# Batched 64x64 matmul on one core: transposing A on VectorE in 32x32 blocks instead of on TensorE

## The chip, the cores and the metric

The kernel runs on one core of one Trainium2 chip. The metric is the device time of one execution in microseconds (us). Three runs of the kernel before gave 134.71, 134.80 and 134.83 us, a median of 134.8 us.

## The reference

1024 independent products of 64x64 matrices in fp32:

```python
a: [1024, 64, 64] float32      # M x K
b: [1024, 64, 64] float32      # K x N
out = np.matmul(a, b)          # [1024, 64, 64] float32
```

16.78 MB of A and 16.78 MB of B are read, and 16.78 MB are written.

## The kernel before

**Tiling.** The work goes in 16 tiles (t) of 64 matrices, each 1 MB of A, of B and of output. A is prepared in 8 superblocks (s) of 128 matrices, so one superblock feeds two tiles. The matrices of a tile are numbered 4g + h, with g from 0 to 15 and h from 0 to 3. Inside the kernel A and B are bf16, and two neighbouring bf16 of A (k = 2kp and 2kp + 1) are moved together as one fp32 word.

**How a product is made.** TensorE multiplies four matrices (h = 0..3) at once: the stationary operand is a block diagonal `at_bd` whose 128 rows are (h, kp) and whose 128 columns are (wl, h', mo), with zeros where h and h' differ. The moving operand is `b_bf`, rows (h, kp), 64 columns. `multiply(t)` (from L158, matmuls at L189) does 64 matmuls a tile: 16 values of g, two of j, and two (u = 0, 1) that add the even and the odd k. Row m of A is m = 4 mo + 2j + wl. Two block diagonals (`N_BD = 2`) take turns; their zeros are written once, one by VectorE (L217), the other in halves by GpSimd (L219, L222).

**How A gets into the block diagonal.** Four steps per superblock:

- `load_a(s)` (L69 to L78): three of the four h are loaded by GpSimd's queue with a cast to bf16 (L73, 128 partitions, 4 KB runs of DRAM, 2 KB in SBUF); the fourth is loaded as fp32 on SP's queue (L77). Superblock 0 comes as fp32 in four parts on SP's and ScalarE's queues (`load_first_a`, L80 to L91).
- `regroup(s)` (L99 to L113): VectorE puts the four h side by side in `a_bf`, one copy of 3072 bf16 (L108) and one cast of 1024 fp32 (L111) per superblock. For s = 0 VectorE and ScalarE share it (L105).
- `transpose(s, j)` (L115 to L126): TensorE transposes 128x128 fp32 words against an identity, four to a PSUM tile (L120), and ScalarE copies each PSUM tile to `at_sb` (L123). That is 16 transposes and 4 copies a superblock.
- `spread(t)` (L128 to L138): VectorE copies 32 partitions at a time from `at_sb` into the block diagonal, 1024 words each (L133), four copies a tile.

**B and the output.** `load_b(t)` (L93 to L97) loads 1 MB of fp32, even tiles on SP's queue, odd ones on ScalarE's, three buffers. `cast(t)` (L140 to L152) makes `b_bf`, two buffers: VectorE does it (L144), except tile 0 (ScalarE) and tile 15 (four pieces, two on each engine, L149 and L151). The products are copied from PSUM to `o_sb` in eight pieces of 64x512 a tile (`evacuate`, L177): ScalarE does all eight on even tiles, six on odd ones, where VectorE does the other two. Tile 15 is done in pieces of 256, half on each engine. `store` (L166) puts 1 MB a tile on GpSimd's queue; tiles 14 and 15 go in pieces on SP's and ScalarE's queues.

**What sets the order.** The order is written out by hand (`manual_schedule`): each engine runs its instructions in the order in which the program names them, and waits at each for what it needs. On VectorE an iteration t is `spread(t+1)`, `cast(t+1)`, then its share of the evacuation and, in every second iteration, `regroup(s+2)`. GpSimd's queue holds the loads of A and the stores in one order; at most eight of its DMAs are outstanding, since each waits for the landing of the one eight before it. A is loaded up to three superblocks ahead (`A_AHEAD = 3`), B three tiles, and a tile is stored one iteration after its evacuation (`HOLD = 2`).

Of the kernel before, what the change touches and what calls it, by code (L numbers as in the profile page):

```python
# [7 lines left out]

fp32 = mybir.dt.float32
# [4 lines left out]
def kernel(  # L14
# [7 lines left out]

    nc = tc.nc
    B, M, K = a.shape  # L30
    _, _, N = b.shape
    assert (M, K, N) == (64, 64, 64) and B % 128 == 0

    n_t, n_s = B // 64, B // 128
    A_AHEAD = 3
    B_AHEAD = 3
    N_BD = 2
    HOLD = 2

    a_v = a.rearrange("(s g h) (mp v) k -> s h g mp (v k)", h=4, g=32, v=16)  # L40
    b_v = b.rearrange("(t g h) (kp u) n -> t (h kp) g (u n)", h=4, g=16, u=2)
# [3 lines left out]
    a_pool = ctx.enter_context(tc.tile_pool(name="a_pool", bufs=A_AHEAD))  # L45
    b_pool = ctx.enter_context(tc.tile_pool(name="b_pool", bufs=B_AHEAD))
    work = ctx.enter_context(tc.tile_pool(name="work", bufs=2))
    o_pool = ctx.enter_context(tc.tile_pool(name="o_pool", bufs=8))
    t_psum = ctx.enter_context(
        tc.tile_pool(name="t_psum", bufs=4, space=bass.MemoryType.PSUM)  # L50
    )
    o_psum = ctx.enter_context(
        tc.tile_pool(name="o_psum", bufs=2, space=bass.MemoryType.PSUM)
    )

    bd_tiles = [
        consts.tile([128, 2, 16, 2, 4, 16], fp32, name=f"at_bd{i}") for i in range(N_BD)
    ]
    identity = consts.tile([128, 128], fp32)
    warm = consts.tile([128, 2], fp32)  # L60
    a_tiles, b_tiles, abf_tiles, at_tiles, bbf_tiles = {}, {}, {}, {}, {}
    held = {}

    def store_queue(t, lo):
        if t < n_t - 2:
            return nc.gpsimd
        return nc.scalar if t == n_t - 1 and lo % 4 == 0 else nc.sync

    def load_a(s):  # L69

        a_sb = a_pool.tile([128, 3, 16, 64], bf16, name="a_sb")
        for h in range(3):
            nc.gpsimd.dma_start(  # L73
                out=a_sb[:, h, :, :].rearrange("p v k -> p (v k)"), in_=a_v[s, h], single_packet=True
            )
        a_raw = a_pool.tile([128, 16, 64], fp32, name="a_raw")
        nc.sync.dma_start(out=a_raw[:].rearrange("p v k -> p (v k)"), in_=a_v[s, 3])  # L77
        a_tiles[s] = a_sb, a_raw  # L78

    def load_first_a():  # L80

        raw = [
            o_pool.tile([128, 8, 2, 2, 64], fp32, name="o_sb")[:].rearrange(
                "p gh j wl n -> p (gh j wl n)"
            )
            for _ in range(2)
        ]
        parts = [raw[h % 2][:, 1024 * (h // 2) : 1024 * (h // 2) + 1024] for h in range(4)]
# [10 lines left out]
    def regroup(s):  # L99
        a_sb = a_tiles.pop(s)  # L100
        a_bf = work.tile([128, 16, 4, 64], bf16, name="a_bf")
        if s == 0:
            for h in range(4):
                copy = nc.scalar.copy if h % 2 else nc.vector.tensor_copy
                copy(a_bf[:, :, h, :], a_sb[h].rearrange("p (v k) -> p v k", v=16))  # L105
        else:
            cast_sb, raw = a_sb
            nc.vector.tensor_copy(  # L108
                a_bf[:, :, 0:3, :], cast_sb[:].rearrange("p h v k -> p v h k")
            )  # L110
            nc.vector.tensor_copy(a_bf[:, :, 3, :], raw[:])  # L111
        abf_tiles[s] = a_bf
        at_tiles[s] = work.tile([128, 2, 32, 2, 4, 4], fp32, name="at_sb")  # L113

    def transpose(s, j):  # L115
        a_cols = abf_tiles[s][:].rearrange("p v h k -> p v (h k)").bitcast(fp32)
        for wl in range(2):
            at_ps = t_psum.tile([128, 4, 128], fp32, name="at_ps")
            for vo in range(4):
                nc.tensor.transpose(  # L120
                    at_ps[:, vo, :], a_cols[:, 4 * vo + 2 * j + wl, :], identity[:]
                )
            nc.scalar.copy(  # L123
                at_tiles[s][:, j, :, wl, :, :],
                at_ps[:].rearrange("p vo (g mp) -> p g mp vo", mp=4),
            )  # L126

    def spread(t):  # L128
        half = slice(16 * (t % 2), 16 * (t % 2) + 16)
        bd = bd_tiles[t % N_BD]  # L130
        for h in range(4):
            rows = slice(32 * h, 32 * h + 32)
            nc.vector.tensor_copy(  # L133
                bd[rows, :, :, :, h, :].rearrange("p j g wl mo -> p j (g wl) mo"),
                at_tiles[t // 2][rows, :, half, :, :, :].rearrange(
                    "p j g wl mp vo -> p j (g wl) (mp vo)"
                ),
            )  # L138

    def cast(t):  # L140
# [15 lines left out]
            piece()  # L156

    def multiply(t):  # L158
        at_bd = bd_tiles[t % N_BD][:].rearrange("p j g wl h mo -> p j g (wl h mo)")
        at_bd = at_bd.bitcast(bf16).rearrange("p j g (c u) -> p j g c u", u=2)  # L160
        b_bf = bbf_tiles.pop(t)
        last = t == n_t - 1
# [6 lines left out]
            )  # L169

        def evacuate(o_ps, gh, n, copies):

            for par in range(2):
                for wl in range(2):
                    src = o_ps[64 * wl : 64 * wl + 64, :, par, :, :]
                    dst = o_sb[64 * par : 64 * par + 64, gh : gh + n, :, wl, :]
                    copies[2 * par + wl](dst, src)  # L177

        for half in range(2):
            if not last:  # L180
                o_ps = o_psum.tile([128, 4, 2, 2, 64], fp32, name="o_ps")
            for g8 in range(8):
                if last and g8 % 4 == 0:
                    o_ps = t_psum.tile([128, 2, 2, 2, 64], fp32, name="at_ps")
                g = 8 * half + g8
                gl = (g8 % 4 if last else g8) // 2
                for j in range(2):
                    for u in range(2):
                        nc.tensor.matmul(  # L189
                            o_ps[:, gl, g % 2, j, :],  # L190
                            at_bd[:, j, g, :, u],
                            b_bf[:, g, 64 * u : 64 * u + 64],
                            start=(u == 0),
                            stop=(u == 1),
                        )
                if last and g8 % 4 == 3:
                    copy = nc.scalar.copy if g8 == 3 else nc.vector.tensor_copy
                    evacuate(o_ps, g // 4 * 2, 2, [copy] * 4)
            if not last:
                copies = [nc.scalar.copy] * 4  # L200
                if half and t % 2:
                    copies[2:] = [nc.vector.tensor_copy] * 2
                evacuate(o_ps, 4 * half, 4, copies)
        if last:
            held[t] = [lambda q=q: put(2 * q, 2) for q in range(4)]
        else:
# [1 line left out]
            held[t] = [lambda q=q: put(q, 8 if whole else 4) for q in ([0] if whole else [0, 4])]  # L208

    with tc.manual_schedule():  # L210
        load_first_a()
# [16 lines left out]
        cast(0)
        for t in range(n_t):
            s, half = t // 2, t % 2  # L230
            if t + 1 < n_t:
                spread(t + 1)
                cast(t + 1)
            if t + B_AHEAD < n_t:
                load_b(t + B_AHEAD)
            if half == 0 and 0 < s < n_s - 1 - A_AHEAD:
                load_a(s + 1 + A_AHEAD)
            if half == 0 and 0 < s < n_s - 1:
                transpose(s + 1, 1)
            multiply(t)  # L240
            if t == 0:
                regroup(1)
                load_a(A_AHEAD)
                load_a(A_AHEAD + 1)
                transpose(1, 0)
                transpose(1, 1)
            elif t == 1:
                regroup(2)
            elif half == 0 and s + 2 < n_s:
                regroup(s + 2)  # L250
            if half == 1 and s + 2 < n_s:
                transpose(s + 2, 0)
# [34 lines left out]
```

## Time and profile before

| what | value |
|---|---|
| median of three runs | 134.8 us |
| span of the profiled execution, first to last instruction | 133.4 us |
| VectorE (DVE) busy | 94.6 us, 71% |
| ScalarE (ACT) busy | 87.9 us, 66% |
| TensorE (PE) busy, of it transposes | 64.4 us, 48%; 21.2 us |
| GpSimd (POOL) busy, mostly issuing DMAs | 33.0 us, 25% |
| DRAM traffic | 33.55 MB read, 16.78 MB written: 377 GB/s over the span |

The page does not give the time of the profiled execution as a run; the 1.4 us between its span and the median of the runs lie before the first and after the last instruction, or are differences between executions.

How to read it: the page gives busy time per engine, the span in 40 slices of 3.3 us with the busy share in tenths, the DMA queues with their packets and bytes, a chain of waits followed back from the last instruction, and the costliest groups of instructions with their mean duration and the idle time before them. DMA bytes are counted as they land, so a load that casts fp32 to bf16 counts half of what it reads. q0 is GpSimd's queue, q1 SP's, q10 ScalarE's. Sizes such as 32x1024 are partitions x elements of one instruction.

### The profile page before, as it was taken

What the parts mean: (1) busy time and instruction counts of PE and PEld (TensorE: products, weight loads), DVE (VectorE), ACT (ScalarE), POOL (GpSimd) and SP (SyncE); (2) the same over time, 40 slices, a digit from 0 to 9 for tenths busy, and PEclk for the clock granted to TensorE, in tenths of its full rate; (3) what the DMA queues carried; (4) which work ended last, traced back from release to release, by engine and by line L of the source; (5) the groups of instructions that cost most, each with busy time, mean ns of one, the idle gap of its engine ahead of it and who ended that gap; (6) DMA issues with size and microseconds to landing.
All of it is one profiled execution on the core that took longest, in us unless ns stands there. A gap on an engine that the chain in (4) does not pass through costs nothing.

```text
span 133.4 us, 2837 instructions
## 1 busy us (share of the span) xinstructions
PE 64.4 (48%) x1152; PEld 61.1 (46%) x1152; DVE 94.6 (71%) x120; ACT 87.9 (66%) x161; POOL 33.0 (25%) x43
## 2 busy tenths in 40 slices
PE   0006406960089384289518970956197363970000
PEld 0006306950089274189418950945196363960000
DVE  5930399109998809995999699959999995987000
ACT  3225424999036998969595969696968969099600
POOL 8991000420090070341233021203020410300000
PEclk9999975797557999856985699599959955599555
DMA  3999999999999999999999999999999999999990
GB/s 77 371 329 311 307 311 281 284 306 325 327 312 401 316 320 333 399 384 397 311 281 375 406 389 351 304 316 390 394 396 387 396 392 391 402 405 398 382 319 18
DMA packets 19021, 45.01 MB, mean 337 GB/s; under 512 B 1088, under 2 KB 3136, under 8 KB 19008
## 3 DMA queue, kind: packets, MB, share of 16 engines
q0 software_dynamic: 6832, 20.19, 50.1%
q1 hardware_dynamic: 7120, 14.68, 30.4%
q10 hardware_dynamic: 5056, 9.96, 19.7%
q8 instruction: 9, 0.15, 0.4%
q14 instruction: 4, 0.03, 0.1%
HBM read 33.55 MB, written 16.78 MB: 377 GB/s over the span
## 4 chain that ended last, share of the span: by engine, by line
DMA 53%; DVE 15%; ACT 13%; PE 6%; issue 5%; SPq 2%; DVEq 0%; ACTq 0%
DMA b_sb<-in_b_dram 53%; ACT o_sb L177 9%; DVE at_bd L133 6%; PE o_ps L189 4%; DVE b_bf L144 4%; DVE o_sb L177 3%; PE at_ps L120 2%; ACT at_sb L123 2%; ACT b_bf L144 1%; SPq L90 1%; DVE a_bf L108 1%; SPq L96 1%; ACT b_bf L151 1%; DVE a_bf L111 0%; SPq L77 0%
## 5 line engine op out<-in xcount | busy, mean ns | idle before, releaser
L177 ACT COPY o_sb<-o_ps 64x512 f32<-64x512 f32 x106 | 61.5, 580 | 10.3 <-PE o_ps L189 9.0
L189 PEld LDWEIGHTS <-at_bd 128*128 128x128 bf16 x1024 | 42.3, 113 | 39.5 <-DVE b_bf L144 25.7
L189 PE MATMUL o_ps<-b_bf,at_bd 128*128 128x64 bf16 x960 | 42.6, 216 | 35.4 <-DVE b_bf L144 23.4
L133 DVE COPY at_bd<-at_sb 32x1024 f32<-32x1024 f32 x64 | 46.9, 733 | 14.1 <-ACT at_sb L123 11.8
L120 PE MATMUL at_ps<-identity,a_bf 128*128 128x128 f32 x128 | 21.2, 335 | 19.4 <-ACT a_bf L105 11.2
L166 POOL DMA_DIRECT2D out_dram<-o_sb x14 | 15.4, 1097 | 56.9 <-ACT at_sb L123 23.4
L120 PEld LDWEIGHTS at_ps<-identity,a_bf 128*128 128x128 f32 x128 | 19.3, 180 | 19.5 <-issue 19.5
L123 ACT COPY at_sb<-at_ps 128x512 f32<-128x512 f32 x32 | 17.5, 590 | 11.0 <-PE at_ps L120 7.8
L144 DVE CAST b_bf<-b_sb 128x2048 bf16<-128x2048 f32 x14 | 17.8, 1271 | 9.6 <-DMA b_sb<-in_b_dram 9.4
L73 POOL DMA_DIRECT2D a_sb<-in_a_dram x21 | 13.6, 662 | 26.4 <-DVE a_bf L108 19.4
L177 DVE COPY o_sb<-o_ps 64x512 f32<-64x512 f32 x14 | 9.7, 690 | 0.3
L108 DVE COPY a_bf<-a_sb 128x3072 bf16<-128x3072 bf16 x7 | 6.7, 950 | 0.0
L105 ACT CAST a_bf<-o_sb 128x1024 bf16<-128x1024 f32 x2 | 2.1, 1044 | 5.2 <-DMA o_sb<-in_a_dram 5.2
L111 DVE CAST a_bf<-a_raw 128x1024 bf16<-128x1024 f32 x7 | 4.8, 683 | 0.0
L144 ACT CAST b_bf<-b_sb 128x2048 bf16<-128x2048 f32 x1 | 1.9, 1900 | 3.9 <-DMA b_sb<-in_b_dram 3.9
L105 DVE CAST a_bf<-o_sb 128x1024 bf16<-128x1024 f32 x2 | 2.8, 1382 | 1.9 <-DMA o_sb<-in_a_dram 1.9
L217 DVE MEMSET at_bd<- 128x4096 f32 x1 | 3.5, 3472 | 0.8 <-issue 0.8
L177 DVE COPY o_sb<-at_ps 64x256 f32<-64x256 f32 x8 | 3.4, 422 | 0.5 <-PE at_ps L189 0.4
L151 ACT CAST b_bf<-b_sb 128x512 bf16<-128x512 f32 x2 | 1.1, 615 | 3.6 <-DMA b_sb<-in_b_dram 3.6
L177 ACT COPY o_sb<-at_ps 64x256 f32<-64x256 f32 x8 | 2.9, 366 | 0.1
L214 ACT ACT_TABLE_LOAD x1 | 1.3, 1283 | 2.3 <-issue 2.3
L189 PE MATMUL at_ps<-b_bf,at_bd 128*128 128x64 bf16 x64 | 2.0, 193 | 1.0 <-DVE at_bd L133 1.0
(12 smaller groups left out, 6.1 us busy)
## 6 DMA issues: line engine op xcount, KB each, us to landing
out_dram<-o_sb POOLq DMA_DIRECT2D x14, 1024.0 KB, 21.6
a_sb<-in_a_dram POOLq DMA_DIRECT2D x21, 256.0 KB, 16.4
a_raw<-in_a_dram SPq DMA_DIRECT2D x7, 512.0 KB, 18.7
o_sb<-in_a_dram SPq DMA_DIRECT2D x2, 512.0 KB, 5.9
o_sb<-in_a_dram ACTq DMA_DIRECT2D x2, 512.0 KB, 7.1
out_dram<-o_sb SPq DMA_DIRECT2D x2, 512.0 KB, 7.5
out_dram<-o_sb SPq DMA_DIRECT2D x2, 256.0 KB, 7.8
out_dram<-o_sb ACTq DMA_DIRECT2D x2, 256.0 KB, 5.5
```

The source lines that it names most:

```text
L73: nc.gpsimd.dma_start(out=a_sb[:, h, :, :].rearrange("p v k -> p (v k)"), in_=a_v[s, h], single_packet=True)
L105: copy(a_bf[:, :, h, :], a_sb[h].rearrange("p (v k) -> p v k", v=16))
L108: nc.vector.tensor_copy(a_bf[:, :, 0:3, :], cast_sb[:].rearrange("p h v k -> p v h k"))
L111: nc.vector.tensor_copy(a_bf[:, :, 3, :], raw[:])
L120: nc.tensor.transpose(at_ps[:, vo, :], a_cols[:, 4 * vo + 2 * j + wl, :], identity[:])
L123: nc.scalar.copy(at_tiles[s][:, j, :, wl, :, :], at_ps[:].rearrange("p vo (g mp) -> p g mp vo", mp=4),)
L133: nc.vector.tensor_copy(bd[rows, :, :, :, h, :].rearrange("p j g wl mo -> p j (g wl) mo"), at_tiles[t // 2][rows, :, half, :, :, :].rearrange(
L144: (nc.vector.tensor_copy if t else nc.scalar.copy)(b_bf[:], b_sb[:])
L166: store_queue(t, lo).dma_start(out=o_v[t, :, lo : lo + n, :], in_=o_sb[:, lo : lo + n].rearrange("p gh j wl n -> p (gh j wl n)"),)
L177: copies[2 * par + wl](dst, src)
L189: nc.tensor.matmul(o_ps[:, gl, g % 2, j, :], at_bd[:, j, g, :, u], b_bf[:, g, 64 * u : 64 * u + 64], start=(u == 0), stop=(u == 1),)
L217: nc.vector.memset(bd_tiles[0][:], 0.0)
```

## The change

The preparation of A is rewritten, for tiles of 64 matrices:

- **Load.** A tile of A lies as 32 partitions (g, mp) for each q (the former h), at partitions 32q to 32q + 31. One partition holds 32 rows of one matrix: an 8 KB run of DRAM, 4 KB in SBUF after the cast. It is loaded with four DMAs of 32 partitions each. Tile 0 comes as fp32 on SP's and ScalarE's queues and is cast by VectorE and ScalarE, one half each; tiles 1 to 15 all come cast, on GpSimd's queue: 60 DMAs, without `single_packet`. Six tiles are kept ahead (`A_AHEAD = 6`, in tiles now).
- **Transpose.** `regroup`, TensorE's 128 transposes, the identity, ScalarE's 32 copies to `at_sb` and the copies of `spread` go. `spread` is now four VectorE transposes a tile, each on 32 partitions and 1024 fp32 words: 32 blocks of 32x32, from `a_sb` directly into the block diagonal. They read runs of 32 words, and write single words: neighbouring words of a block land 32 bytes (mp) or 1 KB (g) apart.
- **Block diagonal.** Its columns are (w, q, mp, vo), and the stationary operand of a matmul is still a run of 128 words.
- **Evacuation.** ScalarE does all eight copies of every tile but the last; VectorE's share on odd tiles goes. `o_ps` has three buffers instead of two; tile 15 uses a pool of its own (`q_psum`).
- **Order.** GpSimd's queue starts with the loads of tiles 1, 2 and 3, and zeroes the second block diagonal between the loads of tiles 3, 4 and 5, each of which waits for a landing of an earlier one. SP's queue no longer carries loads of A after tile 0. In an iteration the order is `spread(t+1)`, `cast(t+1)`, `load_b(t+3)`, `load_a(t+6)`, `multiply(t)`, `store(t-1)`.

```diff
-    n_t, n_s = B // 64, B // 128
-    A_AHEAD = 3
+    n_t = B // 64
+    A_AHEAD = 6
     B_AHEAD = 3
     N_BD = 2
     HOLD = 2
-    a_v = a.rearrange("(s g h) (mp v) k -> s h g mp (v k)", h=4, g=32, v=16)
+    RAW = (0,)
+    a_v = [
+        [
+            a[64 * t + q : 64 * t + 64 : 4].rearrange("g (mp v) k -> g mp (v k)", mp=2)
+            for q in range(4)
+        ]
+        for t in range(n_t)
+    ]
...
-        consts.tile([128, 2, 16, 2, 4, 16], fp32, name=f"at_bd{i}") for i in range(N_BD)
+        consts.tile([128, 16, 4, 4, 2, 8], fp32, name=f"at_bd{i}") for i in range(N_BD)
...
-    def load_a(s):
-
-        a_sb = a_pool.tile([128, 3, 16, 64], bf16, name="a_sb")
-        for h in range(3):
-            nc.gpsimd.dma_start(
-                out=a_sb[:, h, :, :].rearrange("p v k -> p (v k)"), in_=a_v[s, h], single_packet=True
-            )
-        a_raw = a_pool.tile([128, 16, 64], fp32, name="a_raw")
-        nc.sync.dma_start(out=a_raw[:].rearrange("p v k -> p (v k)"), in_=a_v[s, 3])
-        a_tiles[s] = a_sb, a_raw
+    def load_a(t):
+        if t in RAW:
+            raw = raw_pool.tile([128, 32, 64], fp32, name="a_raw")
+            raw_tiles[t] = raw
+        else:
+            a_tiles[t] = a_pool.tile([128, 32, 64], bf16, name="a_sb")
+        for q in range(4):
+            rows = slice(32 * q, 32 * q + 32)
+            if t in RAW:
+                queue = nc.scalar if t == 0 and q % 2 else nc.sync
+                queue.dma_start(
+                    out=raw[rows].rearrange("p v k -> p (v k)"), in_=a_v[t][q]
+                )
+            else:
+                nc.gpsimd.dma_start(
+                    out=a_tiles[t][rows].rearrange("p v k -> p (v k)"),
+                    in_=a_v[t][q],
+                )
...
     def spread(t):
-        half = slice(16 * (t % 2), 16 * (t % 2) + 16)
         bd = bd_tiles[t % N_BD]
-        for h in range(4):
-            rows = slice(32 * h, 32 * h + 32)
-            nc.vector.tensor_copy(
-                bd[rows, :, :, :, h, :].rearrange("p j g wl mo -> p j (g wl) mo"),
-                at_tiles[t // 2][rows, :, half, :, :, :].rearrange(
-                    "p j g wl mp vo -> p j (g wl) (mp vo)"
-                ),
+        pairs = a_tiles.pop(t)[:].rearrange("p v k -> p (v k)").bitcast(fp32)
+        pairs = pairs.rearrange("p (vo w kp) -> p w vo kp", vo=8, w=4)
+        for q in range(4):
+            rows = slice(32 * q, 32 * q + 32)
+            nc.vector.transpose(
+                bd[rows, :, :, q, :, :].rearrange("p g w mp vo -> p w vo g mp"),
+                pairs[rows],
             )
...
-                copies = [nc.scalar.copy] * 4
-                if half and t % 2:
-                    copies[2:] = [nc.vector.tensor_copy] * 2
-                evacuate(o_ps, 4 * half, 4, copies)
+                evacuate(o_ps, 4 * half, 4, [nc.scalar.copy] * 4)
...
+        load_a(3)
+        nc.gpsimd.memset(bd_tiles[1][:, 0:8], 0.0)
+        load_a(4)
+        nc.gpsimd.memset(bd_tiles[1][:, 8:16], 0.0)
+        load_a(5)
+        cast_a(0)
         spread(0)
         cast(0)
         for t in range(n_t):
-            s, half = t // 2, t % 2
             if t + 1 < n_t:
                 spread(t + 1)
                 cast(t + 1)
             if t + B_AHEAD < n_t:
                 load_b(t + B_AHEAD)
...
+            if t + A_AHEAD < n_t:
+                load_a(t + A_AHEAD)
             multiply(t)
```

More of the change, by code (lines that the diff above doesn't have):

```diff
@@ L5 @@
 from concourse import bass_utils, mybir
-from concourse.masks import make_identity
 from concourse._compat import with_exitstack
@@ L31 @@
     _, _, N = b.shape
-    assert (M, K, N) == (64, 64, 64) and B % 128 == 0
-    n_t, n_s = B // 64, B // 128
-    A_AHEAD = 3
+    assert (M, K, N) == (64, 64, 64) and B % 64 == 0
+    n_t = B // 64
+    A_AHEAD = 6
     B_AHEAD = 3
@@ L38 @@
     HOLD = 2
-    a_v = a.rearrange("(s g h) (mp v) k -> s h g mp (v k)", h=4, g=32, v=16)
-    b_v = b.rearrange("(t g h) (kp u) n -> t (h kp) g (u n)", h=4, g=16, u=2)
+    RAW = (0,)
[6 more added lines that the diff above has]
+    ]
+    b_v = b.rearrange("(t g q) (kp u) n -> t (q kp) g (u n)", q=4, g=16, u=2)
     o_v = out.rearrange("(t gh x) (mo w) n -> t (x mo) gh (w n)", gh=8, x=8, w=4)
@@ L45 @@
     a_pool = ctx.enter_context(tc.tile_pool(name="a_pool", bufs=A_AHEAD))
+    raw_pool = ctx.enter_context(tc.tile_pool(name="raw_pool", bufs=2))
     b_pool = ctx.enter_context(tc.tile_pool(name="b_pool", bufs=B_AHEAD))
@@ L48 @@
     o_pool = ctx.enter_context(tc.tile_pool(name="o_pool", bufs=8))
-    t_psum = ctx.enter_context(
-        tc.tile_pool(name="t_psum", bufs=4, space=bass.MemoryType.PSUM)
-    )
-    o_psum = ctx.enter_context(
-        tc.tile_pool(name="o_psum", bufs=2, space=bass.MemoryType.PSUM)
+    o_psum = ctx.enter_context(
+        tc.tile_pool(name="o_psum", bufs=3, space=bass.MemoryType.PSUM)
+    )
+    q_psum = ctx.enter_context(
+        tc.tile_pool(name="q_psum", bufs=2, space=bass.MemoryType.PSUM)
     )
     bd_tiles = [
-        consts.tile([128, 2, 16, 2, 4, 16], fp32, name=f"at_bd{i}") for i in range(N_BD)
+        consts.tile([128, 16, 4, 4, 2, 8], fp32, name=f"at_bd{i}") for i in range(N_BD)
     ]
-    identity = consts.tile([128, 128], fp32)
     warm = consts.tile([128, 2], fp32)
-    a_tiles, b_tiles, abf_tiles, at_tiles, bbf_tiles = {}, {}, {}, {}, {}
-    held = {}
+    a_tiles, raw_tiles, b_tiles, bbf_tiles, held = {}, {}, {}, {}, {}
     def store_queue(t, lo):
@@ L67, in store_queue, with cast_a @@
         return nc.scalar if t == n_t - 1 and lo % 4 == 0 else nc.sync
-    def load_a(s):
-        a_sb = a_pool.tile([128, 3, 16, 64], bf16, name="a_sb")
-        for h in range(3):
-            nc.gpsimd.dma_start(
-                out=a_sb[:, h, :, :].rearrange("p v k -> p (v k)"), in_=a_v[s, h], single_packet=True
-            )
-        a_raw = a_pool.tile([128, 16, 64], fp32, name="a_raw")
-        nc.sync.dma_start(out=a_raw[:].rearrange("p v k -> p (v k)"), in_=a_v[s, 3])
-        a_tiles[s] = a_sb, a_raw
[L80 to L88, printed above, removed]
-        for h in range(4):
-            (nc.scalar if h % 2 else nc.sync).dma_start(out=parts[h], in_=a_v[0, h])
-        a_tiles[0] = parts
+    def load_a(t):
[16 more added lines that the diff above has]
+                )
+    def cast_a(t):
+        a_tiles[t] = a_pool.tile([128, 32, 64], bf16, name="a_sb")
+        raw = raw_tiles.pop(t)
+        if t == 0:
+            nc.vector.tensor_copy(a_tiles[t][:, 0:16, :], raw[:, 0:16, :])
+            nc.scalar.copy(a_tiles[t][:, 16:32, :], raw[:, 16:32, :])
+        else:
+            nc.scalar.copy(a_tiles[t][:], raw[:])
     def load_b(t):
@@ L97, in load_b @@
         b_tiles[t] = b_sb
[L99 to L107, printed above, removed]
-            nc.vector.tensor_copy(
[L109 to L126, printed above, removed]
     def spread(t):
-        half = slice(16 * (t % 2), 16 * (t % 2) + 16)
         bd = bd_tiles[t % N_BD]
-        for h in range(4):
-            rows = slice(32 * h, 32 * h + 32)
-            nc.vector.tensor_copy(
-                bd[rows, :, :, :, h, :].rearrange("p j g wl mo -> p j (g wl) mo"),
-                at_tiles[t // 2][rows, :, half, :, :, :].rearrange(
-                    "p j g wl mp vo -> p j (g wl) (mp vo)"
-                ),
+        pairs = a_tiles.pop(t)[:].rearrange("p v k -> p (v k)").bitcast(fp32)
[5 more added lines that the diff above has]
+                pairs[rows],
             )
@@ L158, in multiply @@
     def multiply(t):
-        at_bd = bd_tiles[t % N_BD][:].rearrange("p j g wl h mo -> p j g (wl h mo)")
+        at_bd = bd_tiles[t % N_BD][:].rearrange("p g (j wl) q mp vo -> p j g (wl q mp vo)", j=2)
         at_bd = at_bd.bitcast(bf16).rearrange("p j g (c u) -> p j g c u", u=2)
@@ L183, in multiply @@
                 if last and g8 % 4 == 0:
-                    o_ps = t_psum.tile([128, 2, 2, 2, 64], fp32, name="at_ps")
+                    o_ps = q_psum.tile([128, 2, 2, 2, 64], fp32, name="q_ps")
                 g = 8 * half + g8
@@ L210 @@
     with tc.manual_schedule():
-        load_first_a()
+        load_a(0)
         nc.vector.memset(warm[:, 0:1], 0.0)
@@ L216 @@
         load_b(1)
+        load_a(1)
         nc.vector.memset(bd_tiles[0][:], 0.0)
-        make_identity(nc, identity)
-        nc.gpsimd.memset(bd_tiles[1][:, 0], 0.0)
-        load_a(1)
         load_b(2)
-        nc.gpsimd.memset(bd_tiles[1][:, 1], 0.0)
         load_a(2)
-        regroup(0)
-        transpose(0, 0)
-        transpose(0, 1)
+        load_a(3)
[4 more added lines that the diff above has]
+        cast_a(0)
         spread(0)
@@ L229 @@
         for t in range(n_t):
-            s, half = t // 2, t % 2
             if t + 1 < n_t:
+                if t + 1 in RAW:
+                    cast_a(t + 1)
                 spread(t + 1)
@@ L235 @@
                 load_b(t + B_AHEAD)
[L236 to L239, printed above, removed]
+            if t + A_AHEAD < n_t:
+                load_a(t + A_AHEAD)
             multiply(t)
[L241 to L252, printed above, removed]
             if t >= HOLD - 1:
```

## The prediction, made before the changed kernel ran

> **What bounds the kernel now.** I read the slices first. The DMA row stands at 9 in all slices but the first and the last, whatever the engines do:
>
> ```profile
> DVE  5930399109998809995999699959999995987000
> ACT  3225424999036998969595969696968969099600
> ...
> DMA  3999999999999999999999999999999999999990
> GB/s 77 371 329 311 307 311 281 284 306 325 327 312 401 316 320 333 399 384 397 311 281 375 406 389 351 304 316 390 394 396 387 396 392 391 402 405 398 382 319 18
> ```
>
> The GB/s look lower in the first half only because a cast load is counted as it lands, at half of what it reads. 50.33 MB of DRAM traffic over the some 127 us in which data flows (from 2.3 to near 130 us) are 396 GB/s, and the stretches without casts show the same 390 to 400. So the transfers are at a limit all the time and no engine is. The queues next:
>
> ```profile
> q0 software_dynamic: 6832, 20.19, 50.1%
> q1 hardware_dynamic: 7120, 14.68, 30.4%
> q10 hardware_dynamic: 5056, 9.96, 19.7%
> ```
>
> Their shares add up to 100.2% of the 16 engines. The chain of waits says the same: 53% of it is a load of B, and between 50 and 112 us the casts of B (L144) start every 6.2 us, five of them after a wait for their landing:
>
> ```profile
> DVE b_bf L144 <- DMA b_sb<-in_b_dram: 9.4, 5, 4.0
> ```
>
> The last stage differs. In stretches over the end (us, busy time of PE, PEld, DVE, ACT, POOL, clock, DMA share, GB/s) the engines stop and then the transfers sag before they end:
>
> ```profile
> 120.00:124.00 4.00, 0.20 (x7) 0.07 (x3) 2.69 (x7) 3.88 (x9) 0.00 (x0) 0.98 1.03 399
> 124.00:126.00 2.00, 0.00 (x0) 0.00 (x0) 0.00 (x0) 1.76 (x5) 0.00 (x0) 0.50 1.06 381
> 126.00:128.00 2.00, 0.00 (x0) 0.00 (x0) 0.00 (x0) 0.00 (x0) 0.00 (x0) 0.50 1.08 378
> 128.00:130.00 2.00, 0.00 (x0) 0.00 (x0) 0.00 (x0) 0.00 (x0) 0.00 (x0) 0.50 0.84 292
> 130.00:132.00 2.00, 0.00 (x0) 0.00 (x0) 0.00 (x0) 0.00 (x0) 0.00 (x0) 0.50 0.11 38
> ```
>
> After 124 us 2.18 MB move in 7.6 us; at 400 GB/s they take 5.5. These **2.1 us** are what the last stores, issued as late as 125.85 us, leave open. Saving engine time is worth that much at most; the rest must come from the transfers themselves.
>
> **The change, part by part.** The rows that price it:
>
> ```profile
> L133 DVE COPY at_bd<-at_sb 32x1024 f32<-32x1024 f32 x64 | 46.9, 733 | 14.1 <-ACT at_sb L123 11.8
> L144 DVE CAST b_bf<-b_sb 128x2048 bf16<-128x2048 f32 x14 | 17.8, 1271 | 9.6 <-DMA b_sb<-in_b_dram 9.4
> L177 DVE COPY o_sb<-o_ps 64x512 f32<-64x512 f32 x14 | 9.7, 690 | 0.3
> L177 DVE COPY o_sb<-at_ps 64x256 f32<-64x256 f32 x8 | 3.4, 422 | 0.5 <-PE at_ps L189 0.4
> ```
>
> *Removed.* TensorE's transposes (21.2 us) and ScalarE's copies to `at_sb` (17.5) lie beside the transfers: nothing on the path. VectorE loses the spreads (46.9), its evacuations on odd tiles (9.7), the regroup (6.7 + 4.8) and 2.1 of the casts of tile 0: 70.2 us.
>
> *Added on VectorE.* 64 transposes of 1024 words. The trace has none, so I bound one by rows. Below: the copy of the same 32x1024 words, 684 ns at its median. Likely: one word at a time. The two PSUM copies above give that rate: (690 - 422)/256 = 1.047 ns a word, and 154 ns fixed, so 1024 words take 1.23 us. Above, far off: GpSimd's select on the identity, 287 ns for 128 words, 2.24 ns a word, or 2.3 us. I take 1.23: the lower end is the rate of another operation that need not reorder anything, the upper one is another engine's, and the PSUM rows are this engine at one word at a time. A tile then costs 4 x (1.23 + 0.02 gap) + 1.26 for its cast of B = **6.27 us**, and VectorE's sum is 94.6 - 70.2 + 78.7 = 103 us, 77% of the span.
>
> [...]
>
> *ScalarE.* 14 more evacuations of 0.58 (+8.1), 17.5 + 1.1 less: 77 us; a tile is 8 x 0.59 = 4.7 us, below VectorE's 6.27. Its cover is the transfers' 7.9 us a tile (3.15 MB at 396 GB/s). TensorE: 43 us.
>
> *Loads of A.* The DMA packets in the trace, by queue and size: a cast packet (4 KB read, 2 KB landed) takes 172 ns, a 4 KB store 168, a 4 KB fp32 load 159 to 176, 2 KB of B 84 to 90, 1 KB 46. A costs 2688 x 172 and 1408 x about 170 ns over 16 engines: 43.9 us. After, per 4 KB read the same 172: 41.3 for 15 tiles and 2.7 for tile 0, 44.0. Casting one share more gains nothing, as the cast costs what it reads. Low end: an 8 KB run goes as one packet; 2 x 84 - 159 = 9 ns saved a packet, 128 packets an engine, -1.1 us. High end: 32 partitions at a time bring every packet from the fastest to the slowest mean of its size, 176/159, +4.7 us. I take -0.6 for packets, and +0.3 for 32 more DMAs (100 instead of 68), each of which ends with a 4-byte packet of 9 ns on every engine (22 at the slow end: 0.7).
>
> [...]
>
> *Order.* In 10 to 17 us the three queues moved 368, 367 and 368 packets: they take turns by packet, with `single_packet` set. Dropping it costs nothing; larger packets of A only shift turns. At the start B's tiles 0 and 1 then land between 17 us (4 KB read a turn: half of 0.4 MB/us for B) and 22 us (8 KB: a third), against 19.3 before; SP's queue now has 0.5 MB of A in front of B instead of 1. GpSimd's new waits for landings (loads of tiles 3 to 5) hold its zeroing of the second block diagonal, 2 x 1.85 us, to about 16 us, so spread(1) ends at 21; behind it wait cast(1) and multiply(1). I take cast(1) at 22 (21.2 before). Stores stay behind loads of A in GpSimd's queue, with eight DMAs outstanding as before; those hold 3.3 MB instead of 5.9, eight microseconds of work: covered.
>
> *The end.* VectorE without waits: 22 + 14 x 6.27 = 110 us for the last cast of B, 116.9 before. Waits for B were 9.4 us; if most of them recur, the last store is issued between 118 and 126, so half of the 2.1 us is regained: -1.0.
>
> **Sum.** 133.4 - 0.6 + 0.3 - 1.0 = 132.1 us of span. The median of the runs stands 1.4 above the span: **133.5 us**.
>
> **The rivals.**
>
> 1. *VectorE becomes the bound through a slow transpose.* From the last cast to the end come 0.85 (casts) + 1 (PE) + 3.5 (evacuation) + 0.4 + 5.5 (landing) + 2.1 = 13.4 us. 22 + 14 x P + 13.4 passes 133.4 at P = 7.0, a transpose of 1.42 us. At 2.3: 7.5 + 16 x 9.28 + 14 x 1.26 + 13.4 = 187, **188 us**. For: scattered writes. [...] Chance 0.15.
> 2. *Narrow loads slow the queues.* Transfers are the bound, so each us is paid: +0.7 to +4.7, **135.5 to 139.5 us**. Chance 0.17.
> 3. *VectorE at 6.27 a tile has no room left.* Waits for B (9.4) and 7 us more in the start, where loads of A take the turns, put the last cast at 126 and the end at 139: **136 to 140 us**. For: without A, transfers need only 5.3 us a tile, so a late VectorE cannot catch up. Against: SP's queue is B's alone, so B comes earlier. Chance 0.12.
> 4. *It is hidden altogether*, same transfers, same sag: **134.6 to 135.0 us**. Chance 0.08.
>
> **How the numbers follow.** The forecast, 132.0 to 134.4, has 0.48. That gives faster 0.48, same 0.08, slower 0.44 (0.2% is about what a measurement of this kernel can tell). The range leaves out rival 1 and the upper edge of rival 3: 131.8 to 139.5. Cases of both signs hold the chance.
>
> **What would show it.** A transpose row of 1.2 to 1.3 us; VectorE near 103 us, ScalarE 77, TensorE 43; the DMA row at 9 to the end, and above 380 GB/s until 128 us. Cast packets well above 172 ns per 4 KB read show rival 2; DMA slices below 9 with VectorE at 9 show rival 1 or 3. A transpose above 1.42 us makes the prediction wrong.

## The result: 166.1 us instead of 134.8, and the profile after

The changed kernel takes **166.06 us** (165.63 to 166.37, four runs) where the kernel before takes 134.81 (134.71 to 134.98, four runs): a ratio of 1.230, 95% interval 1.226 to 1.233. The forecast was 133.5 us in a range of 131.8 to 139.5; it was wrong in sign and size. Where the runs of a kernel lie more than 1.5% apart, as in two of the experiments below, the ratio is that of the faster ones.

The slices of the changed kernel, of 4.1 us each, show that the bound has moved to another engine:

```profile
DVE  6259699799999999999999999999999999999761
ACT  3020015992908274553719091735547290938450
...
DMA  4999999999999999999999999999796882443734
GB/s 114 226 239 238 235 241 236 234 239 272 394 268 374 285 386 286 371 309 349 247 368 229 377 244 353 251 313 388 244 316 193 261 252 88 171 159 105 245 107 152
```

VectorE stands at 9 from 33 us to 152. The DMA row still stands at 9 up to 115 us, but then goes up and down between 2 and 9: the transfers wait for buffers that come free late. The GB/s of the third to the ninth slice stand at 234 to 241, and only a part of the missing rate is the counting of cast loads as they land; more on that below. The queues' shares now add up to 89%:

```profile
q0 software_dynamic: 6688, 22.55, 49.0%
q1 hardware_dynamic: 5920, 10.49, 20.9%
q10 hardware_dynamic: 4864, 9.44, 19.4%
```

The costliest groups, with busy time, mean of one in ns, and idle time before them:

```profile
L110 DVE STREAM_TRANSPOSE at_bd<-a_sb 32x1024 f32<-32x1024 f32 x64 | 123.5, 1929 | 4.1 <-POOL at_bd L194 1.5
...
L84 POOL DMA_DIRECT2D a_sb<-in_a_dram x60 | 35.1, 597 | 54.3 <-DVE at_bd L110 41.1
...
L119 DVE CAST b_bf<-b_sb 128x2048 bf16<-128x2048 f32 x14 | 17.2, 1230 | 0.4
```

One transpose takes **1.93 us, where 1.23 was forecast**. The casts of B (L119), which waited 9.4 us for loads before, have 0.4 us of idle time before them in all. And the loads of A now wait 41.1 us for VectorE to free a buffer. The timeline of VectorE in the middle (start, duration, count) has no gaps:

```profile
65.67 7.85 DVE L110 STREAM_TRANSPOSE at_bd<-a_sb 32x1024 f32<-32x1024 f32 x4
73.55 1.23 DVE L119 CAST b_bf<-b_sb 128x2048 bf16<-128x2048 f32 x1
74.69 7.84 DVE L110 STREAM_TRANSPOSE at_bd<-a_sb 32x1024 f32<-32x1024 f32 x4
82.56 1.23 DVE L119 CAST b_bf<-b_sb 128x2048 bf16<-128x2048 f32 x1
```

A tile costs VectorE 9.0 us. The same timeline gives the whole span: the cast of tile 1 begins at 27.64 us, that of tile 15 at 154.55, 14 tiles of 9.07 later, and the last landing is 10.0 us after that: 164.6. The chain of waits is of no use here. It reaches back over some 5% of the span, to the last transpose, and breaks off there.

### The profile page after: what moved, and what is told of

Same layout as the page of the kernel before. It is cut to its first block, busy times and chain, and to the rows that moved or that the text cites. A ratio compares the mean times of both kernels' runs of the same rounds, so it can differ in the third digit from the quotient of the medians.

```text
span 164.6 us, 2583 instructions
## 1 busy us (share of the span) xinstructions
PE 56.2 (34%) x1024; PEld 53.8 (33%) x1024; DVE 147.9 (90%) x91; ACT 78.3 (48%) x142; POOL 51.5 (31%) x80
## 5 line engine op out<-in xcount | busy, mean ns | idle before, releaser
L110 DVE STREAM_TRANSPOSE at_bd<-a_sb 32x1024 f32<-32x1024 f32 x64 | 123.5, 1929 | 4.1 <-POOL at_bd L194 1.5
L151 ACT COPY o_sb<-o_ps 64x512 f32<-64x512 f32 x120 | 69.6, 580 | 43.8 <-PE o_ps L163 26.4
L163 PEld LDWEIGHTS <-at_bd 128*128 128x128 bf16 x1024 | 53.8, 130 | 105.4 <-DVE b_bf L119 73.9
L163 PE MATMUL o_ps<-b_bf,at_bd 128*128 128x64 bf16 x960 | 52.2, 239 | 98.1 <-DVE b_bf L119 72.0
L84 POOL DMA_DIRECT2D a_sb<-in_a_dram x60 | 35.1, 597 | 54.3 <-DVE at_bd L110 41.1
L141 POOL DMA_DIRECT2D out_dram<-o_sb x14 | 13.0, 928 | 39.6 <-ACT o_sb L151 28.6
L119 DVE CAST b_bf<-b_sb 128x2048 bf16<-128x2048 f32 x14 | 17.2, 1230 | 0.4
L119 ACT CAST b_bf<-b_sb 128x2048 bf16<-128x2048 f32 x1 | 1.9, 1897 | 13.4 <-DMA b_sb<-in_b_dram 13.4
L163 PE MATMUL q_ps<-b_bf,at_bd 128*128 128x64 bf16 x64 | 3.9, 241 | 5.1 <-DVE at_bd L110 4.3
L151 DVE COPY o_sb<-q_ps 64x256 f32<-64x256 f32 x8 | 3.4, 422 | 2.5 <-issue 1.2
L151 ACT COPY o_sb<-q_ps 64x256 f32<-64x256 f32 x8 | 2.9, 367 | 3.4 <-issue 2.2
L192 POOL MEMSET at_bd<- 128x2048 f32 x1 | 1.8, 1824 | 0.0
L194 POOL MEMSET at_bd<- 128x2048 f32 x1 | 1.8, 1824 | 0.0
```

The lines of the kernel that those rows point to most:

```text
L84: nc.gpsimd.dma_start(out=a_tiles[t][rows].rearrange("p v k -> p (v k)"), in_=a_v[t][q],)
L110: nc.vector.transpose(bd[rows, :, :, q, :, :].rearrange("p g w mp vo -> p w vo g mp"), pairs[rows],)
L119: (nc.vector.tensor_copy if t else nc.scalar.copy)(b_bf[:], b_sb[:])
L141: store_queue(t, lo).dma_start(out=o_v[t, :, lo : lo + n, :], in_=o_sb[:, lo : lo + n].rearrange("p gh j wl n -> p (gh j wl n)"),)
L163: nc.tensor.matmul(o_ps[:, gl, g % 2, j, :], at_bd[:, j, g, :, u], b_bf[:, g, 64 * u : 64 * u + 64], start=(u == 0), stop=(u == 1),)
L192: nc.gpsimd.memset(bd_tiles[1][:, 0:8], 0.0)
```

## The experiments

**The theories.** *Scatter* (S in the expectations): a VectorE write of single words far apart costs more than a write next to each other; that makes the 1.93 us, and the 1.93 us make the time. *Narrow loads*: loads of A that cover 32 partitions at a time slow the transfers. *Partitions*: a transpose on 32 of 128 partitions is the slow form. The first kernel puts the forms side by side; the next ones take one suspect away at a time.

**Forms of the transpose, side by side.** `spread` on even tiles is four transposes with different steps between neighbouring words of a block (l is the step in words: 1, 2, 4 and 8); on odd tiles one transpose on 128 partitions and three plain copies. The words land in other places than the products need, so this kernel gives prices and no products.

```diff
+        if t % 2 == 0:
...
+            x = pairs.rearrange("p (h l kp) -> p h l kp", kp=32, l=4)
+            y = f[2].rearrange("p (h x l) -> p h l x", x=32, l=4)
+            nc.vector.transpose(y[r[2]], x[r[2]])
...
+        else:
...
+            nc.vector.transpose(y, x)
...
+            y = f[2].rearrange("p (h x l) -> p h l x", x=32, l=8)
+            nc.vector.tensor_copy(y[r[2]], x[r[2]])
```

> The changed kernel with other instructions in spread; products are wrong, since the words land in other places of the block diagonal. Even tiles: four 32-partition transposes of 1024 words whose neighbouring words land 4, 8, 16 and 32 bytes apart. Odd tiles: one transpose on 128 partitions, 4 bytes apart, and three plain copies of 32x1024 words that write 4, 32 and 16 bytes apart. Theory S (the 1.93 us come from the scattered writes): 4 and 8 bytes 1.23 us, 16 and 32 bytes 1.9 us or more; the copies slow down in the same way, 0.68 at 4 bytes and above 1.0 at 16 and 32. Rival I (a transpose of fp32 words takes 1.7 ns a word wherever it writes): 1.93 us in all four forms and on 128 partitions, the copies 0.68 in all three. No forecast of the total time.

The groups of VectorE by shape. L112, L115, L118 and L121 are transposes that write 4, 8, 16 and 32 bytes apart; L125 is 128 partitions at 4 bytes; L128, L133 and L130 are copies at 4, 16 and 32 bytes:

```profile
L118 DVE STREAM_TRANSPOSE at_bd<-a_sb 32x1024 f32<-32x1024 f32 x8 | 16.1, 2012 | 0.3
L121 DVE STREAM_TRANSPOSE at_bd<-a_sb 32x1024 f32<-32x1024 f32 x8 | 16.1, 2012 | 0.3
L125 DVE STREAM_TRANSPOSE at_bd<-a_sb 128x1024 f32<-128x1024 f32 x8 | 9.9, 1238 | 0.0
L115 DVE STREAM_TRANSPOSE at_bd<-a_sb 32x1024 f32<-32x1024 f32 x8 | 9.9, 1235 | 0.3
L112 DVE STREAM_TRANSPOSE at_bd<-a_sb 32x1024 f32<-32x1024 f32 x8 | 9.8, 1226 | 1.6 <-PE o_ps L183 1.3 <-ACT a_sb L94 0.3
L133 DVE COPY at_bd<-a_sb 32x1024 f32<-32x1024 f32 x8 | 9.2, 1150 | 0.2
L130 DVE COPY at_bd<-a_sb 32x1024 f32<-32x1024 f32 x8 | 8.8, 1104 | 0.3
L128 DVE COPY at_bd<-a_sb 32x1024 f32<-32x1024 f32 x8 | 6.1, 766 | 0.3
```

The price is a step, not a slope: 1226 and 1235 ns up to 8 bytes, 2012 at 16 and at 32. The number of partitions does not matter (1238). Each step had its own group of 32 partitions here; the next kernel has one form on all four groups. Copies pay too (766 against 1104 and 1150; 8 bytes was not tried for them). One run of it took 139.16 us; it mixes all these forms, so the rows tell more than the time.

**Dense writes alone.** Each transpose writes its 1024 words next to each other; the rest is the changed kernel (the products are no longer those of the reference, here and in the next two).

```diff
-        bd = bd_tiles[t % N_BD]
+        flat = bd_tiles[t % N_BD][:].rearrange("p g w q mp vo -> p (g w q mp vo)")
...
-                bd[rows, :, :, q, :, :].rearrange("p g w mp vo -> p w vo g mp"),
-                pairs[rows],
+                flat[rows, 1024 * q : 1024 * q + 1024].rearrange("p (b x) -> p b x", x=32),
+                pairs[rows].rearrange("p (b kp) -> p b kp", kp=32),
```

> The changed kernel, with each transpose writing its 1024 words contiguously (products wrong; instructions, bytes and waits otherwise the same). Theory S: a transpose of 1.23 us, 6.3 us of VectorE a tile, and a time between 133.5 and 139.5 us, the transfers being the bound again, with or without a loss through the narrow loads. Rival I: 1.93 us and 166 us as before this edit.

140.22 us (139.65 to 141.05), ratio to before 1.039 (1.034 to 1.044). Transposes take 1234 ns, VectorE is busy for 103.5 us (103 was forecast), and **25.8 us of the loss are gone**. The kernel is still 5.4 us slower than before, so the scatter is not all. The row of the transposes, and the GB/s of its slices, of 3.5 us:

```profile
L109 DVE STREAM_TRANSPOSE at_bd<-a_sb 32x1024 f32<-32x1024 f32 x64 | 79.0, 1234 | 4.8 <-POOL at_bd L193 1.5
```

```profile
GB/s 92 219 238 237 239 244 241 248 242 243 240 319 385 262 352 334 311 383 291 325 370 278 358 356 299 378 316 342 375 300 371 348 311 402 407 406 366 359 342 115
```

**Dense writes and wide loads.** Tiles 1 to 15 of A come by one cast load of 128 partitions each, the 64 matrices in their order in DRAM.

```diff
+        if t not in RAW:
+            nc.gpsimd.dma_start(
+                out=a_tiles[t][:].rearrange("p v k -> p (v k)"),
+                in_=a[64 * t : 64 * t + 64].rearrange("g (mp v) k -> (g mp) (v k)", mp=2),
+            )
+            return
```

> As the kernel with contiguous transposes, and each tile of A from 1 on loaded by one cast DMA of 128 partitions (64 matrices in order, 8 KB runs, same bytes; products wrong) instead of four of 32 partitions. If narrow loads slow the transfers (rival 2 of the prediction): under theory S 1 to 5 us below the narrow form, and the data rate of the first 25 us rises from some 0.34 to 0.40 MB/us of reading. If they don't: the same time within 0.5 us. Under rival I VectorE sets the time and it stays near 166 us, but the rate in the first 25 us still tells.

136.54 us (136.39 to 136.88), ratio 1.012 (1.009 to 1.014): another 3.7 us. In the fourth to the seventh slice the rate is now 274 to 284 instead of 237 to 244; in the two after these it is nearly the same (250 and 252 against 248 and 242):

```profile
GB/s 80 226 216 274 284 277 281 250 252 302 293 337 354 305 389 280 378 349 305 389 325 328 388 292 378 346 312 382 314 341 371 308 376 397 403 406 384 368 341 68
```

The step changes more than the width: a load takes 64 matrices in order, where it took every fourth, and 15 DMAs take the place of 60. Taking every fourth matrix does not explain it by itself: the kernel before takes every fourth matrix too, over 128 partitions, and from 8 to 14 us it reads 0.40 MB/us (its cast loads counted at what they read), the narrow loads 0.33. The number of DMAs is not parted from the width by any run.

The second and third slice are still low. There tile 0 of A arrives, still on 32 partitions at a time. The next kernel loads it wide as well, in two DMAs:

```diff
+        if t == 0:
+            src = a[0:64].rearrange("g (mp v) k -> (g mp) v k", mp=2)
+            for h, queue in enumerate([nc.sync, nc.scalar]):
+                v = slice(16 * h, 16 * h + 16)
+                queue.dma_start(
+                    out=raw[:, v, :].rearrange("p v k -> p (v k)"),
+                    in_=src[:, v, :].rearrange("p v k -> p (v k)"),
+                )
+            return
```

> As the kernel with contiguous transposes and wide loads, and tile 0 of A too comes by 128 partitions (two DMAs, 4 KB runs) instead of four of 32 (products wrong). If the 1.6 us that the wide kernel still stands above the kernel before come from the narrow fp32 loads of tile 0 at the start, the time falls by 1 to 2 us, to about 135 us, and the first packets of A take about 170 ns per 4 KB instead of 550 to 610 ns per 8 KB. If they come from later stages: no change within 0.4 us.

**133.30 us** (133.26 to 133.44), ratio 0.989 (0.987 to 0.991), 3.2 us less again. That is close to the forecast's 133.5, reached without the scattered writes and without the narrow loads. (Tile 0 also comes in packets of 4 KB here instead of 8, which this kernel does not part from the width.) The second slice has gone from 226 to 338:

```profile
GB/s 81 338 284 280 273 284 251 253 273 310 318 396 259 403 311 338 386 277 376 360 305 381 333 321 391 295 357 368 303 377 339 322 388 393 404 404 404 371 362 102
```

**Wide loads alone.** The changed kernel with its scattered transposes, and the wide cast loads of tiles 1 to 15. This asks whether the parts add up.

```diff
+        if t not in RAW:
+            nc.gpsimd.dma_start(
...
+                in_=a[64 * t : 64 * t + 64].rearrange("g (mp v) k -> (g mp) (v k)", mp=2),
```

> The changed kernel with its scattered transposes, but each tile of A from 1 on loaded by one cast DMA of 128 partitions (64 matrices in order; products wrong). If VectorE alone sets the time of the changed kernel, the narrow loads cost nothing there: 164 to 167 us, the transpose still 1.93 us. If the two costs add up, 3 to 4 us less than the changed kernel: about 162.

166.63 us (166.45 to 166.85), ratio 1.236 (1.233 to 1.238): no gain at all. From 20 to 40 us the data move at 294 GB/s instead of 239, and it is of no use, since VectorE is behind:

```profile
L116 DVE STREAM_TRANSPOSE at_bd<-a_sb 32x1024 f32<-32x1024 f32 x64 | 123.2, 1924 | 3.2 <-PE o_ps L169 1.3
```

So the narrow loads of tiles 1 to 15 cost nothing while the scatter is there, and 3.7 us once it is gone. Tile 0 was not loaded wide beside the scatter.

**Dense transpose, then copies.** This computes the right products: one transpose of 128 partitions a tile into `at_sb`, next to each other, and four VectorE copies into the block diagonal, as before the change.

```diff
+        nc.vector.transpose(
+            at_sb[:].rearrange("p vo w g mp -> p (vo w) (g mp)"),
+            pairs.rearrange("p (b kp) -> p b kp", kp=32),
+        )
...
+            nc.vector.tensor_copy(
+                bd[rows, :, :, q, :, :].rearrange("p g w mp vo -> p g w mp vo"),
+                at_sb[rows].rearrange("p vo w g mp -> p g w mp vo"),
```

> Right products: one transpose a tile on all 128 partitions into a dense tile, then four copies of 32x1024 words into the block diagonal. If a transpose costs the same on 128 partitions as on 32: 1.23 (theory S) or 1.93 us (rival I) + 4 x 0.70 + 1.26 = 5.3 or 6.0 us of VectorE a tile, and 134 to 140 us, bound by the transfers. If the copies pay for reading pairs of words far apart (1.2 us or more each), 8.0 us a tile and some 150 us.

139.27 us (138.88 to 140.38), ratio 1.034 (1.029 to 1.039). The copies read words 512 bytes apart and write runs of sixteen; they cost 1123 ns, where the copy of the same size with both sides next to each other costs 766 above. In return one transpose of 1238 ns serves the whole tile:

```profile
L114 DVE COPY at_bd<-at_sb 32x1024 f32<-32x1024 f32 x64 | 71.9, 1123 | 3.0 <-PE o_ps L167 1.0
...
L108 DVE STREAM_TRANSPOSE at_sb<-a_sb 128x1024 f32<-128x1024 f32 x16 | 19.8, 1238 | 0.4 <-ACT a_sb L94 0.3
```

It does the changed kernel's work 27 us faster, with the same narrow loads.

**The scatter handed to TensorE.** The block diagonal keeps g innermost, the transposes write runs of 16 words, and the matmuls read their weights in steps of 64 bytes.

```diff
-        consts.tile([128, 16, 4, 4, 2, 8], fp32, name=f"at_bd{i}") for i in range(N_BD)
+        consts.tile([128, 4, 4, 2, 8, 16], fp32, name=f"at_bd{i}") for i in range(N_BD)
...
-                bd[rows, :, :, q, :, :].rearrange("p g w mp vo -> p w vo g mp"),
+                bd[rows, :, q, :, :, :].rearrange("p w mp vo g -> p w vo mp g"),
...
-        at_bd = bd_tiles[t % N_BD][:].rearrange("p g (j wl) q mp vo -> p j g (wl q mp vo)", j=2)
-        at_bd = at_bd.bitcast(bf16).rearrange("p j g (c u) -> p j g c u", u=2)
+        at_bd = bd_tiles[t % N_BD][:].bitcast(bf16)
+        at_bd = at_bd.rearrange("p (j wl) q mp vo (g u) -> p j g (wl q mp vo) u", j=2, u=2)
```

> Moves the scatter from VectorE's writes to TensorE's weight reads: the block diagonal keeps g innermost, a transpose writes runs of 16 words (as if its partitions were mp-major; products wrong), and the stationary operand of a matmul is read in steps of 64 bytes instead of 4. If a run of 16 words is enough for VectorE, a transpose takes 1.23 to 1.3 us. If TensorE reads weights 64 bytes apart at the old speed (113 to 130 ns a load), the time is that of the kernel with contiguous transposes, 139 to 141 us. If a weight load doubles or more, TensorE needs 64 x 0.26 = 17 us a tile and the time is above 250 us.

140.43 us (138.88 to 141.12), ratio 1.037 (1.031 to 1.044), the same as dense writes alone. The transposes take 1235 ns, and TensorE pays 166 ns a weight load instead of 125 (dense writes) to 130 (the changed kernel), which lies beside other work:

```profile
L163 PEld LDWEIGHTS <-at_bd 128*128 128x128 bf16 x1024 | 65.3, 166 | 63.4 <-DVE b_bf L119 33.3
```

**The tail of the kernel before.** The prediction counted on 2.1 us that the last stores leave open. Stores held one tile longer in the kernel before:

```diff
-    HOLD = 2
+    HOLD = 3
```

> The kernel before with stores issued one iteration later (HOLD = 3 for 2), everything else the same. The prediction put 2.1 us on the transfers sagging at the end, since the last stores are issued late. If holding stores back lets the last load of B land earlier, the last store is issued earlier and the sag shrinks: 133 to 134.5 us. If the last load of B is not held up by stores, no change, 134.5 to 135.2 us; if the transfers lack work in the middle, 135.5 or more.

135.05 us (134.92 to 135.63), ratio 1.0015 (0.9999 to 1.003): no difference. Holding stores one tile longer does not shorten this tail; other ways to do so were not tried.

**Right products with wide loads.** Two kernels take the layout with g innermost and order the partitions as (q, mp), g beside them, so that one DMA covers all 128. The first has mp = 2 (8 KB runs, one cast load a tile, tile 0 among them):

```diff
+        nc.gpsimd.dma_start(
+            out=a_tiles[t][:].rearrange("p v k -> p (v k)"),
+            in_=a[64 * t : 64 * t + 64].rearrange("(g q) (mp v) k -> (q mp) g (v k)", q=4, mp=2),
+        )
...
```

> Right products from what the runs showed: the block diagonal keeps g innermost (weights read 64 bytes apart), transposes write runs of 16 words, and a tile of A, tile 0 too, comes by one cast DMA on GpSimd's queue whose 128 partitions are (q, mp) times 16 matrices, 8 KB runs. The transposes should take 1.24 us, VectorE 6.3 us a tile. If that DMA moves as fast as the wide one in the order of the matrices: 133 to 134.5 us, below the kernel before. If its 8 outer blocks of 16 partitions bring back the loss of the narrow loads or use only some of the 16 DMA engines: 137 us or more, and the first 25 us show less than 0.4 MB/us read.

The six runs are 145.86, 147.21 and four of 149.93 to 150.32 us; the ratio, 1.086 (1.081 to 1.091), is that of the first two. The profile is of a run of 150.15 us. VectorE waits for A:

```profile
DVE at_bd L102 <- DMA a_sb<-in_a_dram: 23.3, 8, 10.4
```

The loads of A (KB each, median us from issue to landing), here and in the kernel at 133.30 us:

```profile
a_sb<-in_a_dram POOLq DMA_DIRECT2D x16, 512.0 KB, 33.4
```

```profile
a_sb<-in_a_dram POOLq DMA_DIRECT2D x15, 512.0 KB, 15.4
```

So a load takes 33.4 us against 15.4, though both load the same bytes in 8 KB runs. What makes the difference is open. That the load used only some of the 16 DMA engines, as the expectation allows, is not shown: the trace does not name the engine of a packet. The trace also has 144 four-byte packets a load where the other kernel has 16, and no run parts that from the order of the blocks. The second kernel has mp = 4, hence 16 outer blocks of partitions instead of 8, two DMAs a tile, 4 KB runs, and eight transposes of 512 words:

```diff
+        src = a[64 * t : 64 * t + 64].rearrange(
+            "(gh g q) (mp v) k -> gh (q mp) g (v k)", gh=2, q=4, mp=4
+        )
...
```

> Right products, the same idea with 4 KB runs: partitions are 16 (q, mp) blocks of 8 matrices, two cast DMAs of 128 partitions a tile (tile 0 as fp32 on SP's and ScalarE's queues), and eight transposes of 512 words a tile that write runs of 8 words. A transpose of 512 words should take 154 + 512 x 1.05 = 0.69 us, VectorE 8 x 0.71 + 1.23 = 6.9 us a tile, 0.6 more than with 1024 words. If loads are as good as the kernel's before: 133.5 to 136 us; VectorE at 6.9 a tile puts the last cast of B at some 119 us against 117 before, so the upper half is likelier. If runs of 8 words (32 bytes) slow the writes: a transpose above 0.75 us and more than 137 us.

136.90 us (136.45 to 138.33), ratio 1.015 (1.011 to 1.019). A transpose of 512 words takes 681 ns, near the 0.69 us expected. It is the fastest here with the right products and no TensorE transposes, and still 1.5% behind the kernel before. Two kernels ask why. In the first the casts of B of even tiles go to ScalarE; in the second each load takes its 32 matrices in their order in DRAM.

```diff
-            (nc.vector.tensor_copy if t else nc.scalar.copy)(b_bf[:], b_sb[:])
+            (nc.scalar.copy if t % 2 == 0 else nc.vector.tensor_copy)(b_bf[:], b_sb[:])
```

```diff
-        src = a[64 * t : 64 * t + 64].rearrange(
-            "(gh g q) (mp v) k -> gh (q mp) g (v k)", gh=2, q=4, mp=4
-        )
+        src = a[64 * t : 64 * t + 64].rearrange("(gh n) (mp v) k -> gh (n mp) (v k)", gh=2, mp=4)
```

> The kernel of e10 (right products, 4 KB runs, 128 partitions, runs of 8 words), but the casts of B of even tiles go to ScalarE: VectorE 108.6 - 7 x 1.24 = 100 us, ScalarE 78.4 + 7 x 1.9 = 91.7. Theory V (e10's last 2 us over the kernel before come from a VectorE that is busy at 9 tenths from 46 us to 110 and so issues the last stores late): the last store is issued earlier and the time falls by 1 to 2 us, to 135 to 136. Theory Q (they come from the transfers: the order of the packets of A, at 0.37 MB/us at the start, and 3.2 MB that are left after 124 us at only 350 GB/s): 136.5 to 137.5, no change.

> The kernel of e10, but each load of A takes its 32 matrices in their order in DRAM (128 partitions, 4 KB runs, one after the other), so that the wrong matrices are multiplied; the work of all engines is e10's. It differs from e10 in the order of addresses alone. Theory Q, order of addresses: near e5's 133.3, at most 135. Theory R (4 KB runs instead of 8 KB: 172 ns per 4 KB read against 322 per 8 KB, 11 ns a 4 KB for 240 packets an engine, 2.6 us): near e10's 136.9. Theory V (VectorE's 108.6 us): near e10's 136.9 too; e11 parts V from R.

With the casts moved: 137.14 us (136.99 to 137.47), ratio 1.017 (1.015 to 1.019). VectorE is busy for 101.2 us instead of 108.6, and nothing is gained. With the other order of addresses: 134.60 us (134.24 to 134.73), ratio 0.997 (0.996 to 0.998), 2.3 us less with the same instructions on every engine. The GB/s, first with (q, mp) outside, then in order, in slices of 3.4 and 3.3 us:

```profile
GB/s 94 231 253 290 290 272 271 276 290 285 282 274 385 298 343 363 287 389 314 331 376 292 370 345 305 386 316 337 369 288 377 334 314 409 403 385 362 352 342 103
```

```profile
GB/s 99 335 312 307 295 272 280 296 308 300 280 324 372 280 379 345 302 390 319 323 377 293 369 350 306 381 322 317 379 303 363 343 314 405 402 370 361 347 340 115
```

Most of the difference stands in the second to the fourth slice, from 3 to 14 us, when tile 0 and the first cast loads arrive; the 4 KB packets of tile 0 take 286 and 242 ns on SP's and ScalarE's queues in the one, 182 and 177 in the other. Why this order of addresses is slower stays open. No kernel tried here computes the right products faster than the kernel before.

## Why the prediction was wrong, point by point

**The step that failed: "I take 1.23".** In the forms tried, 1024 words go at 1.23 us if they land next to each other or 8 bytes apart; the change writes them 32 bytes and 1 KB apart, and that measured 1.93. Made dense, the same 64 transposes took 25.8 us off the time. The prediction gave its own decision point, 1.42 us, and the true value lay above it. Rival 1 was the right case, at a chance of 0.15 and with a price of 188 us that was too high.

**Why the choice went wrong.** Between 0.684 and 2.3 us the prediction chose by the PSUM rows: copies that read another memory and write runs of 64 words. They gave the price of a word, 1.047 ns, and nothing on the step between written words; no row of the kernel before has a VectorE write of single words far apart. That case stood as rival 1, without a row that priced its step. In the pure forms a transpose costs 1235 ns with steps of 8 bytes and 2012 with steps of 16. The slow price was lower than rival 1 had it: 2.3 us is 1.87 times the 1.23, where the factor measured is 1.64 in the pure forms (2012 to 1226), and 1.57 in the changed kernel (1929 to 1226). Why that kernel's mixed steps cost 1929 ns and not the 2012 of the pure ones is open.

**The sum under rival 1.** With the measured 9.0 us a tile, the prediction's formula gives 22 + 14 x 9.0 + 13.4 = 161.4 us of span; 164.6 were measured. The cast of tile 1 began at 27.64 instead of 22 (+5.6): the transposes of tile 0 take 7.7 us from 10.73, those of tile 1 then wait until GpSimd's zeroing ends at 19.87, some 4 us later than forecast, and take 7.7 as well. From the last cast to the end it is 10.0 instead of 13.4 (-3.4), since the transfers have no backlog left (the last stores land 2.3 to 3.0 us after their issue, where they took 5.5 to 7.8), and 14 tiles at 9.07 give 1.0 more.

**Rival 2 was real as well.** With dense writes, making the loads wide gained 3.7 us in tiles 1 to 15 and 3.2 us in tile 0, in sum 6.9; the bounds were +0.7 to +4.7. How much of it is the width, and how much the number of DMAs and the packet size of tile 0, is open. The prediction asked what a narrow load costs in packets of A. It missed that B's packets suffer beside it: a 2 KB packet of B takes 107 to 110 ns in the changed kernel, 95 to 98 with the wide loads beside the same scatter, and 86 to 90 in the kernel before. It is hidden behind VectorE here.

**What held.** Once scatter and narrow loads are gone, the transfers are the bound (the queues' shares add up to 100.3%), the time is 133.3 against 133.5, and VectorE's sum is 105.0 us (103). ScalarE measured 78.3 us (77). TensorE's 43 us became 56.2: a weight load took 130 ns where it took 111 to 113 before, at a mean granted clock of 0.67 instead of 0.79. The clock does not explain it, for the kernel with the dense transpose and the copies has 126 ns at 0.78; the reason is open.

An 8 KB run is indeed one packet, of 322 ns instead of twice 172. That saves 120 x 22 ns = 2.6 us an engine over 15 tiles, more than the 0.6 that the sum took. The third part of the forecast, 1.0 us from the tail, is there in size. The stretches over the end of the kernel at 133.30 us (columns as in the prediction):

```profile
120.00:124.00 4.00, 1.86 (x32) 1.70 (x31) 0.79 (x2) 2.67 (x8) 0.00 (x0) 0.50 1.02 384
124.00:126.00 2.00, 0.00 (x0) 0.00 (x0) 0.89 (x3) 0.00 (x0) 0.00 (x0) 0.50 1.04 363
126.00:128.00 2.00, 0.00 (x0) 0.00 (x0) 0.00 (x0) 0.00 (x0) 0.00 (x0) 0.50 1.06 364
128.00:130.00 2.00, 0.00 (x0) 0.00 (x0) 0.00 (x0) 0.00 (x0) 0.00 (x0) 0.50 0.56 194
```

After 124 us 1.84 MB move in 5.8 us, where 400 GB/s would take 4.6: by the prediction's own measure 1.2 us are open instead of 2.1, and the last store is issued at 124.9 us instead of 125.85. That the one makes the other is not shown. The 400 GB/s of this measure is not reached in this stage: at a full DMA share it moves 363 and 364 GB/s here, 381 and 378 in the kernel before, and what is left there are almost only the last stores, in packets of 1 KB. Against these rates some 0.8 us are open instead of 1.9.

That the total came out at 133.3 is in part luck. The packets of A and the tail together gave some 3.5 us where the sum had 1.6, the 32 more DMAs that it charged with 0.3 are not there, and the span fell by 2.0 only, from 133.4 to 131.4; where the rest went is open.

## What to carry to other kernels

Here the steps of its operands were part of an instruction's price: before a copy or a transpose is moved to VectorE, look at the step between the words that it writes one after the other (a transpose took 1226 ns at 4 bytes here, 1235 at 8 and 2012 at 16), and time exactly that pattern when no row of the trace shows it. Rows of copies that read another memory did not price it here: they gave 1.23 us, and 1.93 was measured. When a fix for one bound shows no gain, try it again with the other bound gone, as with the wide loads of tiles 1 to 15 here, which were worth nothing and then 3.7 us.

## What the runs showed of the hardware that was not expected

- The write step acts as a threshold between 8 and 16 bytes, for transposes (1226, 1235, 2012, 2012 ns at 4, 8, 16, 32 bytes); copies pay too, by less (766, 1150, 1104 ns at 4, 16, 32; 8 was not tried).
- A VectorE transpose of 128 partitions costs what one of 32 does (1238 against 1226 ns).
- TensorE's weight loads with columns 64 bytes apart take 166 ns, those with columns 4 bytes apart 130 in the changed kernel and 125 with dense writes.
- Beside loads that cover 32 partitions at a time, four to a tile, the other queues' packets are slower as well (B's 2 KB: 107 to 110 ns against 95 to 98 beside one wide load a tile).
- A cast load whose 128 partitions are eight outer blocks of 16 matrices took 33.4 us to land, one of the same size over 128 partitions in order 15.4; what makes the difference is open.
- The order of addresses alone was worth 2.3 us: 136.90 us with 16 blocks of 8 matrices, 134.60 with the matrices in order.
